# The second gate's matrix product as seven quarter products, with weight sums made by accumulating DMAs

## The chip, the cores and the metric

The kernel runs on one core of a Trainium2 chip. A core has a matrix engine (TensorE, PE in the profile, with its weight loads as PEld), three elementwise engines (VectorE = DVE, ScalarE = ACT, GpSimd = POOL) and a queue engine (SyncE = SP) from which most DMAs are issued. Each engine works off its own queue in order, and engines wait for each other by semaphores. The metric is the device time of one launch in microseconds. Three runs of the kernel before took 667.21, 667.22 and 667.36 us; the median is 667.22 us.

## The reference

A trunk of two layers over 512 tokens of width 1024, in fp32. Layer 0 mixes tokens by neighbourhood attention, layer 1 by latent attention (MLA). Behind each mixer and its output projection stands a gated embedding; a last RMSNorm closes the trunk:

```python
    for i in range(DEPTH):
        xn = rmsnorm(x, norm_g[i])
        y = mixer_na(xn, ...) if i % 2 == 0 else mixer_mla(xn, ...)
        h = x + y
        gate = jax.nn.sigmoid(rmsnorm(h, ple_norm[i]) @ ple_w_gate[i])   # 512x1024 @ 1024x1024
        x = h + gate * (p[i] @ ple_w_proj[i])
    return rmsnorm(x, final_norm)
```

The change is about the product inside the sigmoid, in layer 1.

## The kernel before

**Precision.** An fp32 operand is split into a high part (type fp32r) and the rest, and a product is three matmul passes: high·high, low·high, high·low. A weight piece is 128 rows of 1024 columns (512 KB). `load_w` (line 68) brings it in by three steps: a DMA from SP into `wraw` (L77), a conversion on ScalarE into `whi` (L78), a subtraction on POOL into `wlo` (L79). There are three buffers of each, and during an output projection and the gate behind it a further pool of five pairs of `whi` and `wlo`. Tokens are split on ScalarE (L89) and VectorE (L91), out of PSUM.

**Stages.** In order of time: the first norm and the embeddings `pe = p @ ple_w_proj`, kept in DRAM; layer 0's projections and neighbourhood attention (eight pairs of heads; `project(j+1)` is emitted ahead of `attend(j)`); output projection, first gate, norm; layer 1's compressed projections, MLA heads, output projection; the second gate and the last norm.

**Attention of layer 0.** For a pair of heads, q and k weights are loaded and split, 24 matmuls each, and the PSUM result is copied out by ScalarE (L255, L256 for q) and VectorE (L257, L259). Each head loads a bias table of 192 KB from SP (L317). POOL normalises the softmax rows `ex` (L358), which TensorE then transposes (L369, L371); POOL also does one step of each pair's gating (`u`, L198, and `ol`, L202).

**Output projection** (`out_proj`, line 397): two column halves n, four token tiles t of 128, 24 matmuls of 128x512 each. The result is added to the residual (L409), and `turn_h(t, n)` multiplies it by the gate norm's weights, transposes it on TensorE and splits it into `hnT`; behind a tile's second half, the sum of squares (L110 to L112) gives the row factor `rh`.

**Gate** (`gate_phase`, line 465): for each column half n four weight pieces, and for each of four token tiles 24 matmuls into a PSUM bank: 192 matmuls of 128x512. In layer 1 the last tile's block is cut into two of 256 columns. Behind each block: sigmoid on ScalarE with the row factor as scale (L479), times `pe` (L480), plus the residual (L482) on VectorE, then `done`. In layer 1 `done` gathers the last norm's sum of squares (ScalarE L874 and VectorE L875; for the last 256 columns VectorE L870), multiplies the first half by the norm's weights on POOL (L879), and at a tile's second half takes the power on POOL (L882), scales both halves (VectorE L883, ScalarE L884) and stores (L885, L886).

**PSUM** has eight banks by tag: `mm` 2, `S` 2, `T` 3, `O` 1.

**What sets the order.** The program is emitted in source order; a planner that plays it through with costs of its own then orders each engine's queue, within the dependencies. `issue_after(x)` holds what it wraps behind instruction x in that order.

Of the kernel before, what the change touches and what calls it, by code (L numbers as in the profile page):

```python
# [19 lines left out]
P = 128  # L20
S = 512
# [9 lines left out]
NEARLY = 7  # L31

# [7 lines left out]
class Trunk:  # L40
    def __init__(self, tc, ctx, a, dbg=None):
# [12 lines left out]
        self.small = ec(tc.tile_pool(name="small", bufs=8))  # L54
        self.wx, self.wxn = None, 0
        dram = ec(tc.tile_pool(name="dram", bufs=4, space=bass.MemoryType.DRAM))
        self.spill = [dram.tile([P, D], F32, name=f"spill{t}") for t in range(NT)]
        self.pe = [[dram.tile([P, D], F32, name=f"pe{l}{t}") for t in range(NT)] for l in range(2)]

# [8 lines left out]
    def load_w(self, ap, n, extra=False, parts=1, rest=None, late=None):  # L68
# [4 lines left out]
        hi = pool.tile([P, n if extra else 1024], F32R, name="whi", tag="whi", bufs=self.wxn if extra else 3)  # L73
        lo = pool.tile([P, n if extra else 1024], F32R, name="wlo", tag="wlo", bufs=self.wxn if extra else 3)
# [31 lines left out]
    def inv_rms(self, scratch, src, n):  # L106
# [4 lines left out]
        nc.vector.tensor_scalar(ss, ss, 1.0 / n, EPS, op0=ALU.mult, op1=ALU.add)  # L111
# [3 lines left out]
    def rms(self, dst, src, g, n):  # L115
        rs = self.inv_rms(dst, src, n)
        self.nc.vector.scalar_tensor_tensor(dst, src, rs, g, op0=ALU.mult, op1=ALU.mult)
# [95 lines left out]
    def na_heads(self, pool, xT, zs, oT):  # L213
# [99 lines left out]
    def na_head(self, pool, h, sq, s0, dk, kl, vh):  # L313
# [3 lines left out]
        nc.sync.dma_start(bias, self.a["na_bias"][h])  # L317
# [5 lines left out]
        for half in range(2):  # L323
# [31 lines left out]
            for i in range(2):  # L355
                qt = 2 * half + i
                e = ex[:, ecol(qt)]
                nc.gpsimd.tensor_tensor(out=e, in0=e, in1=rc[:, qt:qt + 1].to_broadcast([P, e.shape[1]]), op=ALU.mult)  # L358
# [126 lines left out]

    def mla_c(self, pool, xT, cT, sets):
# [6 lines left out]
        xh, xl = xT  # L493
        L = lambda s, k, t: s[k // 4][:, k % 4, t * P:(t + 1) * P]
        for part, (w0, wn) in enumerate(((0, 384), (384, 288))):
            ws = [self.load_w(a["mla_c"][part][c], 2 * wn, extra=c == 3) for c in range(4)]
            for t in range(NT):
                ps = self.psum(("mm", "mm", "S", "S", "T", "T", "O", "mm")[part * NT + t])
# [5 lines left out]
        for t in range(NT):  # L504
# [255 lines left out]
    def run(self):  # L760
# [7 lines left out]
        with tc.tile_pool(name="pre", bufs=4, reuse_waits="tile") as pool:  # L768
# [36 lines left out]
            nc.gpsimd.tensor_scalar(ss, ss, 1.0 / D, EPS, op0=ALU.mult, op1=ALU.add)  # L805
            nc.gpsimd.tensor_tensor(out=ss, in0=ss, in1=self.half.to_broadcast([P, NT]), op=ALU.pow)
# [16 lines left out]
        x1T = None  # L823
        for layer in range(2):
            with tc.tile_pool(name=f"out{layer}", bufs=4, reuse_waits="tile") as pool:
                self.wx, self.wxn = pool, 5
# [7 lines left out]
                hnT, rh = {}, {}  # L834

# [15 lines left out]
                if layer == 0:  # L851
                    x1T = ([self.bigtile(f"x1h{g}") for g in range(2)], [self.bigtile(f"x1l{g}") for g in range(2)])

                    def done(t, n, o, w):
                        if n == 0:
                            return
# [143 lines left out]
```

## Time and profile before

| | |
|---|---|
| median of the runs | 667.22 us (667.21 to 667.36) |
| span of the profiled execution | 665.9 us |
| TensorE busy | 657.4 us, 99% |
| ScalarE, POOL, VectorE busy | 407.9, 392.8, 354.8 us |
| moved by DMA | 79.09 MB, mean 119 GB/s |
| second gate, first to last matmul | 614.1 to 658.6 us |

The profile is of one execution. Its span runs from the first to the last recorded work; the device time of a run holds a little more. A busy share says how long an engine had an instruction in work. Matmuls overlap in the engine's pipeline, so a single one has a longer duration than the time by which it advances the queue. In the rows of a timeline the columns are the start, the busy time of the group, the engine, the line, the operation, output and inputs, shapes and the count; a bracket at the end tells the idle time before and what ended it. In a DMA group's row the figures are the count of DMAs, the KB of each and the median microseconds from issue to landing.

### The profile page before, as it was taken

To read this page: it belongs to the slowest core of one execution; us is meant where nothing else is said; L and a number is where in the kernel's file an instruction comes from. 1 tells how busy PE (TensorE), PEld (TensorE's weight loads), DVE (VectorE), ACT (ScalarE), POOL (GpSimd) and SP (SyncE) were. 2 spreads that over 40 slices of the span, in tenths; PEclk is the share of its full clock that TensorE was granted. 3 is DMA by queue.
4 is the path that set the end of the run, shared out by engine and by line. 5 is a ranking of instruction groups with operands and counts; after the bars stand their busy time and mean duration, and the time that the engine had idled before them with its cause. 6 is when DMAs were issued, how large, how long until landed. Compare 5 with 4: busy or idle time off the path is not lost.

```text
span 665.9 us, 9961 instructions
## 1 busy us (share of the span) xinstructions
PE 657.4 (99%) x3467; PEld 560.1 (84%) x3467; DVE 354.8 (53%) x794; ACT 407.9 (61%) x812; POOL 392.8 (59%) x320
## 2 busy tenths in 40 slices
PE   9999999999999999999999999999999999999995
PEld 6888888988988888888899888888888888888885
DVE  6280365736645514544625614888988875145234
ACT  7572586857767742543433635898979887436423
POOL 0395466575575765943044626786959786858410
PEclk9999999999999999999999999999999999999999
DMA  9944223222142236534233335120201223664022
GB/s 327 340 153 136 95 87 94 83 85 99 55 150 76 64 133 262 189 105 138 100 104 110 107 89 168 32 74 24 75 23 64 64 96 111 234 240 159 32 80 95
DMA packets 32386, 79.09 MB, mean 119 GB/s; under 512 B 4177, under 2 KB 8785, under 8 KB 32337
## 3 DMA queue, kind: packets, MB, share of 16 engines
q1 hardware_dynamic: 31904, 77.68, 35.0%
q10 hardware_dynamic: 432, 0.79, 0.3%
q8 instruction: 27, 0.44, 0.3%
q14 instruction: 23, 0.18, 0.1%
HBM read 66.92 MB, written 8.39 MB: 113 GB/s over the span
## 4 chain that ended last, share of the span: by engine, by line
PE 95%; DMA 1%; issue 1%; POOL 1%; DVE 0%; ACT 0%; SPq 0%; POOLq 0%; ACTq 0%
PE ps_mm L102 47%; PE ps_S L102 13%; PE ps_mm L550 6%; PE ps_T L128 6%; PE ps_O L661 4%; PE ps_T L102 3%; PE ps_O L102 3%; PE ps_T L227 2%; PE ps_O L383 2%; PE ps_mm L173 2%; PE ps_T L371 2%; PE ps_S L336 1%; PE ps_S L335 1%; PE ps_O L227 1%; DMA qe<-rl 1%
## 5 line engine op out<-in xcount | busy, mean ns | idle before, releaser
L79 POOL TENSOR_TENSOR wlo<-wraw,whi 128x1024 fp32r<-128x1024 f32 (+5 forms) x106 | 208.2, 1980 | 119.2 <-ACT whi L78 91.2
L78 ACT ACTIVATE whi<-wraw 128x1024 fp32r<-128x1024 f32 (+5 forms) x107 | 92.5, 886 | 86.9 <-PE ps_mm L102 17.8
L646 POOL TENSOR_TENSOR ex<-ex,rc 128x512 f32<-128x512 f32 x64 | 66.2, 1044 | 25.2 <-DVE rc L645 18.1
L102 PE MATMUL ps_mm<-whi,hnT 128*128 128x512 f32 (+1 forms) x272 | 70.2, 378 | 0.0
L102 PEld LDWEIGHTS ps_mm<-whi,hnT 128*128 128x128 f32 x272 | 49.3, 188 | 9.2
L644 ACT ACTIVATE ex<-ps_S,mx 128x512 f32<-128x512 f32 x64 | 44.0, 688 | 11.9 <-DVE mx L642 10.8
L642 DVE TENSOR_REDUCE mx<-ps_S 128x1 f32<-128x512 f32 x64 | 43.7, 683 | 6.9 <-PE ps_S L102 6.2
L91 DVE TENSOR_TENSOR pt_lo<-ps_T,pt_hi 128x512 fp32r<-128x512 f32 x64 | 43.3, 682 | 7.7 <-ACT pt_hi L89 7.3
L358 POOL TENSOR_TENSOR ex<-ex,rc 128x128 f32<-128x128 f32 (+1 forms) x64 | 34.1, 561 | 20.9 <-DVE rc L354 20.9
L102 PE MATMUL ps_mm<-xh,whi 128*128 128x512 f32 x152 | 40.8, 399 | 0.0
L102 PE MATMUL ps_mm<-wlo,hnT 128*128 128x512 f32 (+1 forms) x136 | 40.5, 378 | 0.0
L89 ACT ACTIVATE pt_hi<-ps_T 128x512 fp32r<-128x512 f32 x64 | 37.7, 594 | 4.4 <-PE ps_T L128 4.1
L128 PE MATMUL ps_T<-ident,ex 128*128 128x128 f32 x256 | 38.4, 272 | 0.0
L102 PE MATMUL ps_mm<-xl,whi 128*128 128x512 f32 x152 | 38.2, 390 | 0.0
L102 PE MATMUL ps_mm<-xh,wlo 128*128 128x512 f32 x152 | 38.0, 390 | 0.0
L128 PEld LDWEIGHTS ps_T<-ident,ex 128*128 128x128 f32 x256 | 31.5, 140 | 7.7 <-POOL ex L646 0.4
L102 PEld LDWEIGHTS ps_mm<-xl,whi 128*128 128x128 f32 x152 | 28.4, 188 | 5.8
L102 PEld LDWEIGHTS ps_mm<-xh,wlo 128*128 128x128 f32 x152 | 28.3, 188 | 5.8
L194 DVE TENSOR_TENSOR u<-ps_O,u 64x512 f32<-64x512 f32 x32 | 22.0, 687 | 19.9 <-ACT u L193 19.3
L112 POOL TENSOR_TENSOR rs<-ss,half 128x1 f32<-128x1 f32 x20 | 12.7, 637 | 33.7 <-DVE ss L111 33.6
L480 DVE TENSOR_TENSOR sg<-pe,sg 128x512 f32<-128x512 f32 (+1 forms) x17 | 12.4, 728 | 35.8 <-ACT sg L479 35.8
L352 ACT ACTIVATE ex<-ex,mx 128x128 f32<-128x128 f32 (+1 forms) x64 | 30.3, 474 | 1.9 <-DVE mx L342 1.0
(354 smaller groups left out, 1644.6 us busy)
## 6 DMA issues: line engine op xcount, KB each, us to landing
pe<-pe SPq DMA_DIRECT2D x32, 256.0 KB, 2.8
wraw<-na_qk SPq DMA_DIRECT2D x16, 512.0 KB, 3.3
wraw<-gate SPq DMA_DIRECT2D x16, 512.0 KB, 3.4
wraw<-na_v SPq DMA_DIRECT2D x8, 512.0 KB, 3.3
wraw<-na_o SPq DMA_DIRECT2D x8, 512.0 KB, 3.5
wraw<-mla_z SPq DMA_DIRECT2D x8, 512.0 KB, 3.5
wraw<-mla_o SPq DMA_DIRECT2D x8, 512.0 KB, 3.6
wraw<-na_z SPq DMA_DIRECT2D x6, 512.0 KB, 5.4
```

The lines of the kernel that those rows point to most:

```text
L78: nc.scalar.activation(hi[:, c], raw[:, c], AF.Copy)
L79: f = lambda e, c=c: e.tensor_tensor(out=lo[:, c], in0=raw[:, c], in1=hi[:, c].bitcast(F32), op=ALU.subtract)
L89: self.last_copy = nc.scalar.activation(hi, src, AF.Copy, scale=scale)
L91: nc.vector.tensor_tensor(out=lo, in0=src, in1=hi.bitcast(F32), op=ALU.subtract)
L102: last = self.last_mm = nc.tensor.matmul(out, l, r, start=i == 0, stop=i == n - 1)
L128: self.last_mm = self.nc.tensor.transpose(t[:, i * P:(i + 1) * P], b, self.ident)
L352: self.last_exp = nc.scalar.activation(e, e, AF.Exp, scale=-1.0, bias=mx[:, qt:qt + 1], accum_out=sm[:, qt:qt + 1])
L358: nc.gpsimd.tensor_tensor(out=e, in0=e, in1=rc[:, qt:qt + 1].to_broadcast([P, e.shape[1]]), op=ALU.mult)
L550: self.last_mm = nc.tensor.matmul(PS[key], *terms[i], start=i == 0, stop=i == len(terms) - 1)
L642: nc.vector.reduce_max(mx, sp, axis=AX.X, negate=True)
L644: nc.scalar.activation(ex, sp, AF.Exp, bias=mx, accum_out=sm)
L646: nc.gpsimd.tensor_tensor(out=ex, in0=ex, in1=rc.to_broadcast([P, S]), op=ALU.mult)
```

## The change

With `SEVEN = (1,)` the second gate's product is computed as in Winograd's form of Strassen's method. Tokens (rows, two halves of 256), the inner dimension and the columns are halved; of the eight products of quarters seven remain, of sums of quarters. Numbered 1 to 7 in the code, they run in the order 1, 7, 6, 5, 4, 3, 2. Each is two row halves of 128 with 12 matmuls of 128x512 (inner dimension 512, three passes): 168 in place of 192. For products 1 and 2 the second row half is cut into 256-column pieces.

- **Weight sums.** Products 4 to 7 use sums of weight quarters. Four copies of 1 MB within DRAM (`sums_begin`, SP queue) stand behind a bias load in the first heads of layer 0's attention, and four accumulating DMAs of 1 MB (`sums_add`, issued by POOL, rows of 1 KB) behind normalisations in the next head pairs. The gate then loads 14 pieces of 512 KB (8 before): 14 conversions on ScalarE, 14 subtractions on POOL.
- **Token mixes.** `turn_h` multiplies by a row factor too (`rows`, from tiny operations on POOL and one reciprocal). `keep_half` takes the transposed halves from PSUM: it keeps copies, forms sums and differences of quarters on VectorE, and `operand` splits each of the 14 row halves into high and low part.
- **Partial results.** Products 5 and 3 accumulate in the banks of product 6, and product 2 in those of product 1; ScalarE copies the results of 1 and 6 out in between (`s1`, `s6`), VectorE forms `s17`, and POOL makes two subtractions on `s6`. The blocks behind products 5, 4 and 3 start with one VectorE sum.
- **Order.** The output projection's second half takes the token tiles as 0, 2, 1, 3. The gate's blocks end in another order: tiles 2 and 3 with column half 1, then 0; tiles 0 and 1 with half 1, then 0, so that `done` now takes the halves in the order in which they come. The extra pool holds five pairs under one tag.

```diff
+    def sums_begin(self, layer):
+        q = lambda n, c: self.a["gate"][layer, n, c:c + 2].rearrange("c p n -> (c p) n")
+        w = self.quarter[layer] = {1: q(0, 0), 2: q(0, 2), 3: q(1, 2), "f": q(1, 0)}
+        for p, src in ((7, "f"), (5, 1), (6, 1), (4, 2)):
+            nc.sync.dma_start(t[p], w[src])
+    def sums_add(self, layer, step):
+        for p, src in {0: ((7, q[3]), (5, q["f"])), 1: ((6, t[7]),), 2: ((4, t[6]),)}[step]:
+            self.nc.gpsimd.dma_start(t[p], src, accum_op=ALU.add, max_dma_last_dim=1024)
...
             attend(j)
+            for l in SEVEN:
+                if j == 0:
+                    with self.tc.issue_after(self.last_bias.ins):
+                        self.sums_begin(l)
+                elif j < 4:
+                    with self.tc.issue_after(self.last_norm.ins):
+                        self.sums_add(l, j - 1)
...
+    def operand(self, p, i, x, lo=None):
+        nc.scalar.activation(t[:, i, :], x, AF.Copy)
+        (lo or nc.vector).tensor_tensor(out=t[:, 2 + i, :], in0=x, in1=t[:, i, :].bitcast(F32), op=ALU.subtract)
...
+    def keep_half(self, t, n, ps):
+        i = t % 2
+        ac, c = self.F[:, i, :], self.F[:, 2 + i, :]
+        if t < 2:
+            self.operand(1 + n, i, ps)
+            nc.scalar.activation(self.B[i] if n else ac, ps, AF.Copy)
+        elif n == 0:
+            nc.scalar.activation(c, ps, AF.Copy)
+            nc.vector.tensor_tensor(out=ac, in0=ac, in1=ps, op=ALU.subtract)
+            self.operand(7, i, ac)
+        else:
+            nc.vector.tensor_tensor(out=ac, in0=ac, in1=ps, op=ALU.add)
+            nc.vector.tensor_tensor(out=c, in0=c, in1=ps, op=ALU.subtract)
+            nc.scalar.activation(self.Dd[i], ps, AF.Copy)
+    def mixed(self, p):
+        for i in range(2):
+            if p == 3:
+                self.nc.vector.tensor_tensor(out=self.B[i], in0=self.B[i], in1=self.F[:, i, :], op=ALU.subtract)
+            self.operand(p, i, {6: self.F[:, i, :], 5: self.F[:, 2 + i, :], 3: self.B[i], 4: self.Dd[i]}[p])
...
+    def gate_seven(self, pool, layer, rh, res, after):
+        order = (1, 7, 6, 5, 4, 3, 2)
+        for p in order[:3]:
+            prep(p)
+        self.mixed(6)
+        for k, p in enumerate(order):
+            if k + 3 < len(order):
+                prep(order[k + 3])
+            if 0 < k < 4:
+                self.mixed(order[k + 2])
+            for i in range(2):
+                cuts = parts if layer == 1 and i == 1 and p < 3 else whole
...
+                    m = [(x[:, 2 * s + i, k * P:(k + 1) * P], W[p][k // 2][r][:, k % 2 * S + o:k % 2 * S + o + wd])
+                         for c in range(2) for s, r in ((0, 0), (1, 0), (0, 1)) for k in (2 * c, 2 * c + 1)]
+                    for j, (l, r) in enumerate(m):
+                        nc.tensor.matmul(ps[:, :wd], l, r, start=j == 0 and p in (1, 7, 6, 4),
+                                         stop=j == 11 and p not in (1, 6, 5), skip_group_check=True)
+                    if p == 1:
+                        nc.scalar.activation(s1[i][:, o:o + wd], ps[:, :wd], AF.Copy)
+                    elif p == 2:
+                        finish(i, 0, pool.tile([P, S], F32, name="g", tag="hg", bufs=3)[:, :wd], ps[:, :wd], o, wd)
+                    elif p == 7:
+                        nc.vector.tensor_tensor(out=s17[i], in0=ps, in1=s1[i], op=ALU.add)
+                    elif p == 6:
+                        nc.scalar.activation(s6[i], ps, AF.Copy)
+                    elif p == 5:
+                        quarter(2 + i, 1, ps, s17[i], ALU.subtract)
+                        nc.gpsimd.tensor_tensor(out=s6[i], in0=s17[i], in1=s6[i], op=ALU.subtract)
+                    elif p == 4:
+                        quarter(2 + i, 0, ps, s6[i], ALU.add)
+                    else:
+                        quarter(i, 1, ps, s1[i], ALU.subtract)
...
-            for t in range(NT):
-                ps = self.psum(("mm", "mm", "S", "S", "T", "O", "mm", "mm")[n * NT + t])
+            for u, t in enumerate((0, 2, 1, 3) if n and self.wxn > 5 else range(NT)):
+                ps = self.psum(("mm", "mm", "S", "S", "T", "O", "mm", "mm")[n * NT + u])
```

More of the change, by code (lines that the diff above doesn't have):

```diff
@@ L31 @@
 NEARLY = 7
+SEVEN = (1,)
 def win(t, r0, r1, off, dims):
@@ L54, in __init__ @@
         self.small = ec(tc.tile_pool(name="small", bufs=8))
+        self.rows = [[self.const.tile([P, NT], F32, name=f"row{n}{l}") for n in "abcd"] for l in range(2)]
         self.wx, self.wxn = None, 0
@@ L58, in __init__ @@
         self.pe = [[dram.tile([P, D], F32, name=f"pe{l}{t}") for t in range(NT)] for l in range(2)]
+        self.quarter = {}
+        self.sums = [{p: dram.tile([2 * P, D], F32, name=f"sum{l}{p}") for p in (4, 5, 6, 7)} for l in range(2)]
     def bigtile(self, name):
@@ L503, in mla_c @@
         slab_l = pool.tile([P, S], F32R, name="slab_l", tag="slab", bufs=2)
-        for t in range(NT):
+        for t in toks:
             c = cs[t]
@@ L851, in run @@
                 if layer == 0:
-                    x1T = ([self.bigtile(f"x1h{g}") for g in range(2)], [self.bigtile(f"x1l{g}") for g in range(2)])
                     def done(t, n, o, w):
-                        if n == 0:
+                        if t not in seen:
+                            seen.add(t)
                             return
```

159 lines of the change are left out of this document (129 added, 30 removed).

## The prediction

> **What bounds the kernel now.** I read the page first (span, busy shares, chain), then the chain in order of time for the end, then a window over the second gate.
>
> ```profile
> span 665.9 us, 9961 instructions
> PE 657.4 (99%) x3467; PEld 560.1 (84%) x3467; DVE 354.8 (53%) x794; ACT 407.9 (61%) x812; POOL 392.8 (59%) x320
> PE 95%; DMA 1%; issue 1%; POOL 1%; DVE 0%; ACT 0%; SPq 0%; POOLq 0%; ACTq 0%
> ```
>
> TensorE is busy 99% of the span and is 95% of the chain; the other engines stand near 55%. So what counts is matmul time, and any hole that new work tears into it.
>
> ```profile
> 621.06 31.78 PE ps_mm L102 x140
> 655.10 0.73 ACT sq L874 x2
> 656.70 3.88 issue
> 661.19 0.75 DVE r L883
> ```
> ```profile
> core 0: us, PE busy (x) PEld busy (x) DVE busy (x) ACT busy (x) POOL busy (x), PEclk, DMA share, GB/s
> 5.00:15.00 10.00, 9.70 (x42) 7.66 (x42) 9.80 (x16) 9.07 (x16) 0.00 (x0) 1.00 1.04 377
> 52.00:66.00 14.00, 14.00 (x64) 11.58 (x63) 0.00 (x0) 3.46 (x4) 7.57 (x4) 1.00 0.40 135
> 614.11:658.60 44.49, 44.46 (x221) 37.64 (x219) 16.58 (x32) 16.92 (x32) 13.66 (x11) 1.00 0.19 66
> ```
>
> The chain's long row gives 31.78/140 = 0.227 us for one matmul of 128x512 in the second gate. The last window is that gate up to its last matmul: TensorE 44.46 of 44.49 us, granted clock 1.00, VectorE, ScalarE and POOL busy 17, 17 and 14 us. The end is a chain from the last matmul (658.6) to 665.9, 7.3 us. The profiled run spans 665.9, and the median of the runs is 667.2, so I add 1.3 us to a span.
>
> **The change part by part.**
>
> *Matmuls.* Eight tokens-by-half blocks of 24 become seven products of two row halves with 12 each: 192 → 168. The blocks cut into 256 columns make up one whole block's length before (24 pairs) and the same after (two blocks of 12 pairs), so they cancel. 24 × 0.227 = **−5.45 us**, all of it on the path.
>
> *End.* The rows after the last matmuls:
>
> ```profile
> 655.10 0.63 ACT L874 ACTIVATE sq<-r 128x512 f32<-128x512 f32 x1 [1.54 <-DVE r L482]
> 655.63 0.19 ACT L874 ACTIVATION_READ_ACCUMULATOR sq<-r 128x1 f32 x1
> 656.73 0.73 ACT L884 ACTIVATE r<-r,rs 128x512 f32<-128x512 f32 x1 [0.52 <-POOL rs L882]
> 656.73 0.75 DVE L883 SCALAR_TENSOR_TENSOR r<-r,rs,gn 128x512 f32<-128x512 f32 x1
> 658.61 0.47 ACT L479 ACTIVATE sg<-ps_mm,rs 128x256 f32<-128x256 f32 x1 [0.19 <-PE ps_mm L102]
> ```
>
> The last block's own steps (L479 onward) are unchanged. Before it, the neighbour token's block ended 24 matmuls (5.4 us) earlier, now 12 (2.7 us), so its square (0.63 + 0.19) can sit in ScalarE's queue ahead of the last sigmoid. I take that one square, **+0.8 us**. Bounds: 0 if it is through in time, 2.3 if the neighbour's scaling (0.73, 0.75) stands there as well.
>
> *The four 1 MB copies in DRAM.* They are issued on SP in the first layer's attention, behind the second head's bias and so ahead of weights: three before the k weights of head pair 0, one before the q weights of pair 1.
>
> ```profile
> 46.13 0.33 SPq L77 DMA_DIRECT2D wraw<-na_qk  x1
> 46.68 1.28 SPq L317 DMA_DIRECT2D bias<-na_bias  x3
> wraw<-na_qk SPq DMA_DIRECT2D x16, 512.0 KB, 3.3
> spill<-r SPq DMA_DIRECT2D x4, 512.0 KB, 2.7
> qo<-rl SPq DMA_DIRECT2D x8, 64.0 KB, 2.0
> 64.64 1.06 ACT L78 ACTIVATE whi<-wraw 128x1024 fp32r<-128x1024 f32 x1 [4.38 <-PE ps_O L227]
> 71.84 0.59 ACT L255 ACTIVATE sa<-ps_mm 64x512 fp32r<-64x512 f32 x1 [0.43 <-PE ps_mm L102]
> 73.79 0.69 DVE L259 SCALAR_TENSOR_TENSOR sb<-ps_mm,sb 64x512 fp32r<-64x512 f32 x1
> 77.08 1.98 PE L102 MATMUL ps_mm<-xh,whi 128*128 128x512 f32 x8
> ```
>
> 448 KB more take 1.3 us more: 345 GB/s, and 1.8 us fixed. Call a copy c. If one queue is served in order, pair 1's q weights land at 47.5 (after two of the bias issues) + 1.1 (two bias tables, 0.56 each) + 4c + 1.5 (k weights) + 0.56 (third table) + 1.5 + 1.8 = 54.0 + 4c. Their conversion ran at 64.64 and may slip about 3.0 us: behind it on ScalarE stand 0.43 us of idle time and the steps that empty a PSUM bank, done at 74.48, wanted at 77.08. So the deadline is 67.7, met up to c = 3.4. No copy within DRAM is in the trace. Lower end c = 3.0 (1 MB at 345 GB/s; 377 in the first window when all engines are full): nothing late. Upper end 6.1 (reading and writing in turn): 78.4, 10.7 us of idle TensorE. [...] In all, the loss is 4(c − 3.4).
>
> [...]
>
> *The four accumulating DMAs* are issued by POOL: two behind the pair of ex rows that ends at 117.48, one at 128.4, one at 156.9. POOL's queue stands still while it writes their 1024 rows each.
>
> ```profile
> 116.29 1.19 POOL L358 TENSOR_TENSOR ex<-ex,rc 128x256 f32<-128x256 f32 x2
> 118.37 2.40 POOL L79 TENSOR_TENSOR wlo<-wraw,whi 128x1024 fp32r<-128x1024 f32 x1 [0.89 <-ACT ph L89]
> 122.37 0.97 POOL L358 TENSOR_TENSOR ex<-ex,rc 128x128 f32<-128x128 f32 x2 [1.60 <-DVE rc L354]
> 124.79 0.27 PE L369 MATMUL ps_T<-ident,ex 128*128 128x128 f32 x1
> 130.62 1.29 POOL L198 TENSOR_TENSOR u<-u,z 128x512 f32<-128x512 f32 x1 [2.21 <-DVE u L194]
> 132.87 1.30 POOL L202 TENSOR_TENSOR ol<-u,oh 128x512 fp32r<-128x512 f32 x1 [0.96 <-ACT oh L201]
> 160.08 1.01 POOL L358 TENSOR_TENSOR ex<-ex,rc 128x128 f32<-128x128 f32 x2 [0.80 <-DVE rc L354]
> 164.40 0.27 PE L369 MATMUL ps_T<-ident,ex 128*128 128x128 f32 x1
> ```
>
> Behind the pair stand wlo, then the ex that TensorE transposes at 124.79; its slack is 0.89 + 1.60 + 1.45 = 3.9 us. Behind the third stand u and ol (2.21 + 0.96 = 3.2 us); behind the fourth the ex that ends at 161.09 and is transposed at 164.40 (0.80 + 3.3 = 4.1 us). An SP issue of 128 rows takes 0.33 us; with the same for any DMA the pair is 0.7, with one such step for each 128 rows 2.6 each and 5.2 for the pair, 1.3 us too long. I take 0 with 1.3 kept; a gain is excluded, as this is work added. Their transfers run on a queue of their own, and weight conversions there wait for TensorE's buffers, not for loads:
>
> ```profile
> L78 ACT ACTIVATE whi<-wraw 128x1024 fp32r<-128x1024 f32 (+5 forms) x107 | 92.5, 886 | 86.9 <-PE ps_mm L102 17.8
> ```
>
> *Weights and mixes in the gate.* Fourteen weight pieces for eight, and more operand work.
>
> ```profile
> 593.73 11.85 POOL L79 TENSOR_TENSOR wlo<-wraw,whi 128x1024 fp32r<-128x1024 f32 x5 [1.60 <-ACT whi L78]
> 618.61 2.39 POOL L79 TENSOR_TENSOR wlo<-wraw,whi 128x1024 fp32r<-128x1024 f32 x1
> 624.12 1.29 POOL L879 TENSOR_TENSOR r<-r,gn 128x512 f32<-128x512 f32 x1 [3.12 <-ACT sq L874]
> 639.63 1.28 POOL L879 TENSOR_TENSOR r<-r,gn 128x512 f32<-128x512 f32 x1 [4.16 <-ACT sq L874]
> L91 DVE TENSOR_TENSOR hnT<-ps_T,hnT 128x512 fp32r<-128x512 f32 x4 | 2.7, 688 | 2.9 <-ACT hnT L89 2.9
> L89 ACT ACTIVATE hnT<-ps_T 128x512 fp32r<-128x512 f32 x4 | 2.3, 587 | 0.0
> ```
>
> POOL: 6 × 2.39 + 2 subtractions × 1.28 = 17 us more. VectorE: 22 more half-tile steps (6 low parts, 8 mixes, 8 sums behind products) × 0.69 = 15 us. ScalarE: 19 copies (14 of token operands, 5 of products) × 0.59, and 6 more weight pieces × 1.06 = 18 us. On top of 14, 17 and 17 us that makes 31, 32 and 35 in about 39 us of matmuls, and part runs ahead during the output projection. POOL is the tightest: before, eight pieces were through at 621.0. Six more end no sooner than 621.0 + 14.3 + 2.6 + 4 × 1.28 = 643.0; the last product starts at 614.1 + 6 × 5.45 = 646.8. The third product's operands, the first that need mixes after the last transposes, have two products (10.9 us) for about four VectorE and three ScalarE steps (4.5 us). I take 0; bounds 0 and, if POOL stayed 4 us idle more than I count, some 3 us.
>
> **Sum.** −5.45 + 0.8 + 1.1 + 0 + 0 = −3.55: span 662.35, time **663.7 us**.
>
> **The rivals.**
>
> *A, the other side: the copies are slow.* The deadline of pair 1's q weights decides: the loss 4(c − 3.4) eats the 4.65 us left above c = 4.6. At the upper end, 6.1, it is 10.7: 673.3 us. For it: nothing shows both sides of a copy overlapping. Against: loads of whole tiles and the spill to DRAM are both under 3.5 us for 512 KB. Chance 0.20, more than half of it close to the point of decision. [...]
>
> *B, POOL writes descriptors slowly.* With G for each DMA the stalls are 2G − 3.9, G − 3.2 and G − 4.1, together 4G − 11.2; beside the copies' 1.1 the gain is gone from G = 3.7. At G = 5, 8.8 us: 672.5. Nothing speaks for it but that no such DMA is in the trace; against it the 0.33 us row. Chance 0.08.
>
> *C, the gate starves.* The change does not do what it says: the 24 matmuls leave, but the products wait for POOL's pieces. If none ran ahead, 14 × 2.39 + 2.6 + 5.1 = 41.2 us against 38.1 of matmuls, +3.1: 666.8. Against: POOL's rows at 593.73. Chance 0.10.
>
> **How the numbers follow.** The forecast's case holds 0.62, its own range 661.8 (no tail, copies hidden) to 666.0 (tail 2.3, copies at c = 3.9). Measured runs differ by 0.02%; 0.2% (1.3 us) is about what can be told from no change. Faster: 0.62 and a little of C, 0.64. Same: parts of A and C, 0.11. Slower: the rest of A and B, 0.25. The range 661.5 to 669.0 takes in C and A up to c = 5.0, and leaves out A's far end and B's, about 0.16.
>
> **What would show it.** Gate: 168 whole matmuls' worth, TensorE without holes. Tail: 8.1 us after the last matmul. Copies: their landing, and TensorE idle between 77 and 90 us (pair 1) if c is over 3.4. POOL: length of its DMA issues, transposes late after 118, 129 and 160 us. I am wrong if the 5.45 us is there in the gate and lost in the first 170 us.

## The result, and the profile after

| | before | changed |
|---|---|---|
| median of the runs | 667.22 us (667.21 to 667.36) | 670.1 us (669.8 to 670.96) |
| ratio to before | | 1.0045 [1.0031, 1.0059] |
| span of the profiled execution | 665.9 us | 668.0 us |
| second gate, first to last matmul | 614.1 to 658.6 us | 613.6 to 653.6 us |
| from the last matmul to the end | 7.3 us | 14.4 us |

The change makes the kernel slower by 0.45%; 663.7 us was predicted. The gate's last matmul ends 5.0 us earlier, and the kernel ends 2.1 us later: what follows the last matmul has grown by 7.1 us. The profiled execution of the changed kernel took 669.8 us, 1.8 us more than its span; it is the shortest of four, whose spans run from 668.0 to 669.2 us. The medians lie 2.9 us apart, these two spans 2.1.

The page of the changed kernel, its busy shares, and windows over the gate and its end:

```profile
PE 652.5 (98%) x3443; PEld 555.5 (83%) x3443; DVE 383.1 (57%) x817; ACT 422.3 (63%) x837; POOL 421.4 (63%) x340
PE 91%; DVE 2%; POOL 2%; issue 2%; DMA 1%; ACT 1%; POOLq 0%; DVEq 0%
```
```profile
614.00:630.00 16.00, 15.90 (x84) 13.29 (x83) 15.90 (x17) 11.39 (x21) 13.38 (x6) 1.00 0.50 171
630.00:640.00 10.00, 10.00 (x46) 8.28 (x45) 3.04 (x5) 6.57 (x9) 8.57 (x5) 1.00 0.24 86
640.00:650.00 10.00, 9.88 (x44) 7.87 (x43) 9.02 (x11) 4.27 (x9) 5.37 (x4) 1.00 0.19 65
650.00:656.00 6.00, 3.61 (x28) 3.29 (x26) 5.77 (x12) 4.89 (x11) 2.92 (x4) 1.00 0.42 147
656.00:662.00 6.00, 0.00 (x0) 0.00 (x0) 5.96 (x13) 3.16 (x9) 3.74 (x3) 0.55 0.26 96
```

The columns of the windows are those of the prediction's: TensorE, weight load, VectorE, ScalarE, POOL. TensorE is busy 35.78 of the 36 us from 614 to 650 at a granted clock of 1.00, so it isn't starved. VectorE (third figure) is busy only 3.04 of the 10 us between 630 and 640, and then almost without a gap to 662, when TensorE has long ended. On the chain TensorE fell from 95% to 91%; VectorE rose from 0 to 2% and POOL from 1 to 2%.

VectorE's groups from 589 us to the end, shapes kept apart, show why its row is so long:

```profile
L539 DVE TENSOR_TENSOR X<-mix,X 128x512 fp32r<-128x512 f32 x6 | 9.1, 1523 | 2.0 <-ACT X L538 2.0
L599 DVE TENSOR_TENSOR r<-r,g 128x512 f32<-128x512 f32 x7 | 8.2, 1177 | 0.0
L1016 DVE SCALAR_TENSOR_TENSOR hg<-r,rowb,gp 128x512 f32<-128x512 f32 x5 | 5.7, 1152 | 2.2 <-PE ps_T L139 2.2
L604 DVE TENSOR_TENSOR g<-ps_S,s 128x512 f32<-128x512 f32 x4 | 2.7, 681 | 4.6 <-PE ps_S L634 4.6
L560 DVE TENSOR_TENSOR mix<-mix,ps_T 128x512 f32<-128x512 f32 x2 | 1.4, 680 | 2.1 <-PE ps_T L139 2.1
```

All are steps over one 128x512 tile. Those with an operand from PSUM (`ps_S`, `ps_T`) take 0.68 us; the three groups whose two large operands lie in SBUF take 1.15 to 1.5 us on the average. From 640 on six of them are long, and each of the six meets a POOL step. VectorE's rows first, then POOL's:

```profile
640.75 1.02 DVE L597 TENSOR_TENSOR g<-pe,g 128x512 f32<-128x512 f32 x1 [3.08 <-ACT g L594]
641.81 2.77 DVE L599 TENSOR_TENSOR r<-r,g 128x512 f32<-128x512 f32 x1
646.03 1.22 DVE L597 TENSOR_TENSOR g<-pe,g 128x512 f32<-128x512 f32 x1 [0.19 <-ACT g L594]
650.85 1.12 DVE L599 TENSOR_TENSOR r<-r,g 128x512 f32<-128x512 f32 x1
656.38 1.63 DVE L599 TENSOR_TENSOR r<-r,g 128x512 f32<-128x512 f32 x1
659.54 1.42 DVE L599 TENSOR_TENSOR r<-r,g 128x256 f32<-128x256 f32 x1
```
```profile
639.94 1.28 POOL L650 TENSOR_TENSOR s<-s,s 128x512 f32<-128x512 f32 x1
641.18 2.85 POOL L590 TENSOR_TENSOR wlo<-wraw,whi 128x1024 fp32r<-128x1024 f32 x1
645.41 1.29 POOL L1064 TENSOR_TENSOR r<-r,gn 128x512 f32<-128x512 f32 x1 [1.38 <-ACT sq L1060]
649.95 1.47 POOL L1064 TENSOR_TENSOR r<-r,gn 128x512 f32<-128x512 f32 x1 [3.25 <-ACT sq L1060]
655.98 1.49 POOL L1064 TENSOR_TENSOR r<-r,gn 128x512 f32<-128x512 f32 x1 [2.32 <-ACT sq L1060]
658.91 1.77 POOL L1064 TENSOR_TENSOR r<-r,gn 128x512 f32<-128x512 f32 x1 [1.44 <-ACT sq L1060]
```

Each of the six steps from 640.75 to 659.54 begins while POOL has one in work, and ends 0.3 to 0.6 us behind POOL's end. Against 0.68 us (0.41 for the 256-column one) they cost 0.34 + 2.09 + 0.54 + 0.44 + 0.95 + 1.01 = 5.4 us, on an engine that has hardly any idle time left. That is one part of the 7.1 us. The other is that VectorE starts late:

```profile
636.99 0.69 DVE L604 TENSOR_TENSOR g<-ps_S,s 128x512 f32<-128x512 f32 x1 [4.64 <-PE ps_S L634]
```
```profile
637.62 1.06 ACT L589 ACTIVATE whi<-wraw 128x1024 fp32r<-128x1024 f32 x1 [3.40 <-POOL s L650]
638.70 1.28 ACT L594 ACT_TABLE_LOAD   x1
640.00 0.72 ACT L594 ACTIVATE g<-g,rs 128x512 f32<-128x512 f32 x1
```

The first sum behind a product starts at 636.99, after 4.64 us of waiting for TensorE: the planner put half of product 4 ahead of product 5. Then the first sigmoid stands behind the last weight conversion and a table load until 640.00. By then 13.6 us of matmuls are left, and all eight blocks of outputs are still to be multiplied and added.

### The profile page after: what moved, and what is told of

Its sections match the earlier page's. It is cut to its first block, busy times and chain, and to the rows that moved or that the text cites. A ratio compares the mean times of both kernels' runs of the same rounds, so it can differ in the third digit from the quotient of the medians.

```text
span 668.0 us, 10021 instructions
## 1 busy us (share of the span) xinstructions
PE 652.5 (98%) x3443; PEld 555.5 (83%) x3443; DVE 383.1 (57%) x817; ACT 422.3 (63%) x837; POOL 421.4 (63%) x340
## 4 chain that ended last, share of the span: by engine, by line
PE 91%; DVE 2%; POOL 2%; issue 2%; DMA 1%; ACT 1%; POOLq 0%; DVEq 0%
PE ps_mm L107 42%; PE ps_S L107 13%; PE ps_mm L721 6%; PE ps_T L139 6%; PE ps_O L832 4%; PE ps_T L107 3%; PE ps_O L107 3%; PE ps_T L238 2%; PE ps_O L402 2%; PE ps_mm L184 2%; PE ps_T L390 2%; PE ps_S L354 1%; PE ps_S L353 1%; DVE r L599 1%; PE ps_O L238 1%
## 5 line engine op out<-in xcount | busy, mean ns | idle before, releaser
L84 POOL TENSOR_TENSOR wwlo<-wraw,wwhi 128x1024 fp32r<-128x1024 f32 (+5 forms) x93 | 178.6, 1934 | 106.3 <-ACT wwhi L83 91.4
L83 ACT ACTIVATE wwhi<-wraw 128x1024 fp32r<-128x1024 f32 (+5 forms) x94 | 79.1, 863 | 74.4 <-PE ps_mm L107 18.3
L107 PE MATMUL ps_mm<-xh,wwhi 128*128 128x512 f32 x152 | 40.9, 399 | 0.0
L590 POOL TENSOR_TENSOR wlo<-wraw,whi 128x1024 fp32r<-128x1024 f32 x14 | 36.4, 2619 | 3.2 <-ACT whi L589 3.2
L107 PE MATMUL ps_mm<-xl,wwhi 128*128 128x512 f32 x152 | 38.3, 391 | 0.0
L107 PE MATMUL ps_mm<-xh,wwlo 128*128 128x512 f32 x152 | 38.0, 390 | 0.0
L107 PE MATMUL ps_mm<-wwhi,hnT 128*128 128x512 f32 x128 | 35.0, 392 | 0.0
L107 PEld LDWEIGHTS ps_mm<-xl,wwhi 128*128 128x128 f32 x152 | 28.4, 188 | 5.9
L370 ACT ACTIVATE ex<-ex,mx 128x128 f32<-128x128 f32 (+1 forms) x64 | 30.2, 474 | 1.8 <-DVE mx L360 0.8
L107 PE MATMUL ps_S<-ke,qe 96*128 96x512 f32 x96 | 28.9, 407 | 0.0
L107 PE MATMUL ps_S<-ko,qo 128*128 128x512 f32 x96 | 28.9, 409 | 0.0
```

Of the source, the lines that this page charges most:

```text
L83: nc.scalar.activation(hi[:, c], raw[:, c], AF.Copy)
L84: f = lambda e, c=c: e.tensor_tensor(out=lo[:, c], in0=raw[:, c], in1=hi[:, c].bitcast(F32), op=ALU.subtract)
L107: last = self.last_mm = nc.tensor.matmul(out, l, r, start=i == 0, stop=i == n - 1)
L590: nc.gpsimd.tensor_tensor(out=lo, in0=raw, in1=hi.bitcast(F32), op=ALU.subtract)
```

## The experiments

Two theories stood at first. **P**: VectorE and POOL hold each other up when both read SBUF, and that stretches the end. **Q**: VectorE's steps are long for a reason of their own (their tiles, their waits). The expectations also name **N**: the number of blocks that are left for the last 17 us. Out of it came **O**: the order of the products, which starts the blocks late.

### The two engines alone

A kernel of its own with nothing but rows of steps on VectorE and POOL over tiles in SBUF and PSUM, of which this is the core; it computes nothing of the reference.

```python
section(2, 12, 6, dss, gtt)   # VectorE: two SBUF operands; POOL: 128x1024 subtraction
section(3, 24, 7, dps, gtt)   # VectorE: one operand in PSUM; the same POOL row
section(5, 24, 7, dss, gset)  # POOL only writes
section(6, 24, 24, dss, lambda o, f: gtt(o, f, 256))
```

> A kernel of its own that computes nothing of the reference: VectorE and POOL run additions and subtractions on fixed tiles, in sections. Theory P (VectorE and POOL exclude each other while a VectorE instruction reads two SBUF tiles and a POOL instruction reads SBUF): VectorE 128x512 from two SBUF tiles takes 0.69 us alone and about 2.4 us beside POOL's 128x1024 subtraction, 1.3 beside POOL's 128x512, about 0.7 to 0.8 beside POOL's 128x256; with one operand in PSUM 0.69 throughout; beside a POOL memset 0.69. Rival Q (the rows of the changed kernel are long for another reason, such as a wait for data that the record counts as busy): 0.69 in all sections.

Its timeline, with rows of VectorE and then of POOL:

```profile
10.25 16.09 DVE L38 TENSOR_TENSOR d<-x,x 128x512 f32<-128x512 f32 x7
26.97 3.59 DVE L41 TENSOR_TENSOR d<-pt,x 128x512 f32<-128x512 f32 x5
38.60 0.68 DVE L38 TENSOR_TENSOR d<-x,x 128x512 f32<-128x512 f32 x1
```
```profile
11.42 13.65 POOL L47 TENSOR_TENSOR p<-x,x 128x1024 f32<-128x1024 f32 x5
27.76 9.60 POOL L47 TENSOR_TENSOR p<-x,x 128x1024 f32<-128x1024 f32 x4
```

Beside POOL's subtraction a step of VectorE with two SBUF operands takes 16.09 / 7 = 2.30 us on the average, alone 0.68. The average takes in the first step, beside a shorter POOL step, and the last, which begins behind POOL's row; the five between them take 2.71 us each. One of the five, and the POOL step beside it:

```profile
16.91 2.67 POOL L47 TENSOR_TENSOR p<-x,x 128x1024 f32<-128x1024 f32 x1
17.41 2.71 DVE L38 TENSOR_TENSOR d<-x,x 128x512 f32<-128x512 f32 x1
```

VectorE's step ends 0.54 us behind POOL's, as in the changed kernel. With one operand in PSUM a VectorE step takes 0.69 us beside the same row, and POOL 2.40 us (9.60 / 4, whether or not VectorE is at work) instead of 2.73 (13.65 / 5). So the two take turns by whole instructions in these rows, and P holds; Q, which gave 0.69 in every section, falls. Beside POOL's steps of 512 and of 256 columns VectorE took 1.63 and 1.1 us, more than the 1.3 and the 0.7 to 0.8 expected.

### The copies and the accumulating DMAs alone

The kernel before, with `sums_begin` and `sums_add` and their calls added; their sums are not used.

```diff
+            for l in SEVEN:
+                if j == 0:
+                    with self.tc.issue_after(self.last_bias.ins):
+                        self.sums_begin(l)
+                elif j < 4:
+                    with self.tc.issue_after(self.last_norm.ins):
+                        self.sums_add(l, j - 1)
```

> The kernel before with the four copies and the four accumulating DMAs added at the places of the change, and their sums not used. Theory H (hidden): span 665.9 us, first gate and second gate as before. Theory K (the DMAs cost a part of the 2.9 us): TensorE idle near 77 us or near 118 to 160 us. The changed kernel's runs are 1.8 to 2.1 us longer than their spans and those of before 1.3; if the DMAs issued by POOL are the reason, this kernel takes 667.7 us with a span of 665.9, and if not, 667.2.

Measured: 667.64 us against 667.66, ratio 1.0001 [0.9992, 1.001], span 665.9. All eight DMAs cost nothing that can be told. The 7 us are not theirs. The kernel before had a median span of 665.9 us beside it, so it too took 1.8 us more than its span here: the DMAs issued by POOL are not the reason for such a difference, and the 1.3 us that the prediction added is no constant.

### POOL's subtractions left out, or cut

First the 14 low parts are left out, and the matmuls read the high part in their place:

```diff
-                nc.gpsimd.tensor_tensor(out=lo, in0=raw, in1=hi.bitcast(F32), op=ALU.subtract)
-                W[p].append((hi, lo))
+                W[p].append((hi, hi))
```

> The changed kernel without POOL's 14 subtractions for low parts of the gate's weights; the matmuls read the high part in their place (a wrong product, as many matmuls). Theory P (POOL's long instructions hold up VectorE's): VectorE's steps between two SBUF tiles in the gate fall from 1.2 to 1.7 us to 0.69, the end after the last matmul from 14.5 to 8 to 9 us: 664 us. Theory N (not the neighbour but the number: seven of eight blocks end in the gate's last 17 us, with 20 us of VectorE work at 0.69): the end stays at 11 us or more: 667 us or more. Both: between.

Then they stay, each cut into four of 256 columns, so that a VectorE step has a shorter POOL step beside it:

```diff
-                nc.gpsimd.tensor_tensor(out=lo, in0=raw, in1=hi.bitcast(F32), op=ALU.subtract)
+                for s in [slice(i * 256, (i + 1) * 256) for i in range(4)]:
+                    nc.gpsimd.tensor_tensor(out=lo[:, s], in0=raw[:, s], in1=hi[:, s].bitcast(F32), op=ALU.subtract)
```

> The changed kernel with each of POOL's 14 subtractions in the gate cut into four of 256 columns, the result unchanged. Theory P: a VectorE step waits for at most one short POOL instruction, some 0.7 us in place of 2.4; about half of the gap to the kernel without them comes back, 666 to 668 us. Theory N: no change, 670 us, or slower by POOL's fixed cost for each of 42 more instructions.

Left out: 667.96 us, ratio 1.0005 [0.9996, 1.0015], span 666.5, the end 12.7 us. That is 1.7 us of the 7.1 us: P alone had expected 664 us and an end of 8 to 9 us, N 667 us or more and an end of 11 us or more, as measured. VectorE's first sum still starts at 638.24, and POOL's `r` times `gn` still meets VectorE's steps: two sums with the residual (L598) take 2.38 us from 646.89 on, beside a POOL step from 647.26 to 648.72.

Cut: 676.03 us, ratio 1.0131 [1.0114, 1.0148], worse, and outside what either theory gave (666 to 668, or 670 us). Rows of the timeline, of VectorE, POOL and TensorE, and then a window behind them:

```profile
643.43 4.86 DVE L598 TENSOR_TENSOR g<-pe,g 128x512 f32<-128x512 f32 x1 [6.59 <-ACT g L595]
642.18 5.56 POOL L591 TENSOR_TENSOR wlo<-wraw,whi 128x256 fp32r<-128x256 f32 x8
649.67 2.08 PE L635 MATMUL ps_S<-whi,X 128*128 128x512 f32 x4 [4.95 <-DVE g L605]
```
```profile
650.00:656.00 6.00, 6.00 (x15) 4.65 (x15) 5.61 (x10) 2.99 (x7) 2.58 (x2) 0.51 0.32 106
```

A single VectorE step stood 4.86 us, from the second of POOL's eight short steps to the end of the eighth: VectorE didn't get in between them here, though it did in the kernel of the two engines alone (1.1 us a step). What decides that is open. TensorE then waited 4.95 us for a PSUM bank, and afterwards ran at a granted clock of 0.51 for 6 us, with 15 matmuls in that window.

### One cause at a time, with POOL at work

Three single edits of the changed kernel, and all three together. The blocks behind products 4, 3 and 2 keep their values in the PSUM bank of their product, so that VectorE reads one operand from PSUM:

```diff
-            x = pool.tile([P, S], F32, name="g", tag="hg", bufs=3)
+            x = pool.tile([P, S], F32, name="g", tag="hg", bufs=3) if keep else ps
...
-                        finish(i, 0, pool.tile([P, S], F32, name="g", tag="hg", bufs=3)[:, :wd], ps[:, :wd], o, wd)
+                        finish(i, 0, ps[:, :wd], ps[:, :wd], o, wd)
```

> The changed kernel with the blocks behind products 4, 3 and 2 kept in their PSUM banks: the sum, the sigmoid and the product with pe are written over the bank, so that none of these VectorE steps reads two SBUF tiles (product 5's two blocks stay as they are). Theory P: the product and residual rows of these blocks go from 0.8 to 1.2 us to 0.69, some 4 us off VectorE's row of work at the end, ratio to before about 0.999. Theory N (VectorE's number of steps and their late start): under 1 us, ratio 1.003 to 1.0045.

The products are held in their order 1, 7, 6, 5, 4, 3, 2:

```diff
+                        with self.tc.issue_after(prev) if prev is not None and j == 0 else nullcontext():
+                            mm = nc.tensor.matmul(ps[:, :wd], l, r, start=j == 0 and p in (1, 7, 6, 4),
...
+                    prev = mm.ins
```

> The changed kernel with TensorE's products held in the order 1, 7, 6, 5, 4, 3, 2 (in the changed kernel the planner put half of product 4 ahead of product 5, and began 6 ahead of 7). Theory N: product 5's first block ends near 633 us in place of 636.8, VectorE's last row of work starts up to 4 us earlier and ends as much earlier: ratio 0.999 to 1.001. Theory P: no change, 1.0045, or worse if the mixes of product 5 come too late. Theory W (the first sigmoid waits in ScalarE's queue behind the last weight conversion, whose load waits for POOL): the first sum is earlier and the first sigmoid is not, still near 640 us: 1.003 to 1.0045.

The table of the sigmoid is loaded early, by a tiny sigmoid behind the first copy of product 1:

```diff
+                        if i == 0:
+                            with self.tc.issue_after(cp.ins):
+                                nc.scalar.activation(self.small.tile([P, 1], F32, name="dm", tag="dm", bufs=1), self.half, AF.Sigmoid)
```

> The changed kernel with one sigmoid of 128x1 right behind the copy of product 1's first half, so that the table load of 1.28 us falls there and not ahead of the first block's sigmoid. If VectorE's wait for that sigmoid (3.08 us in the changed kernel) passes on to the end, 1.2 us less: ratio 1.0025. If not, 1.0045.

And the three edits together:

> The three edits together: blocks in PSUM, the order held, the table loaded early; result unchanged. If the causes add, 3 to 4 us + 0 to 4 + 1.2 of the 7.2 us that the end is longer than before come back: ratio 0.993 to 0.997. If all of them shorten the same wait, as one of them alone.

| | median, us (before beside it) | ratio | span, us | last matmul ends | end, us |
|---|---|---|---|---|---|
| blocks in PSUM | 669.11 (667.89) | 1.0019 [1.0009, 1.0028] | 666.8 | 653.7 | 13.1 |
| order held | 673.53 (667.89) | 1.0079 [1.0062, 1.0096] | 672.5 | 661.2 | 11.3 |
| table early | 674.31 (667.89) | 1.0098 [1.0083, 1.0113] | 672.5 | 658.2 | 14.3 |
| all three | 671.33 (667.89) | 1.0051 [1.0036, 1.0066] | 669.7 | 658.0 | 11.7 |

Only the first helps, by less than the 4 us that P gave: its end is 13.1 us. With the order held the end does become shorter, 11.3 us in place of 14.4, but the last matmul comes 7.6 us later: product 5 comes earlier than its operands, which VectorE forms beside POOL. A row of VectorE, the row of TensorE that waits for it, and a window:

```profile
634.50 2.25 DVE L539 TENSOR_TENSOR X<-mix,X 128x512 fp32r<-128x512 f32 x1
634.04 1.22 PE L636 MATMUL ps_S<-whi,X 128*128 128x512 f32 x2 [3.50 <-DVE X L539]
```
```profile
630.00:640.00 10.00, 6.50 (x17) 4.78 (x16) 10.00 (x8) 4.59 (x6) 9.30 (x5) 0.66 0.35 107
```

VectorE is busy all 10 us and TensorE waits 3.50 us for it, again followed by a lower clock: 0.66 over the window, and 0.43 us for a matmul from 634.04 to 640.01, where it took 0.23 before the wait. The planner's own order had covered this lateness. With the early table, the load stands at 631.50 ahead of two weight conversions in ScalarE's queue, and the first sigmoid starts at 644.03, later than without. Its gate also began 3 us later, at 616.56, and so did that of the three edits together; TensorE's rows are a little slower there from about 270 us on: 1700 matmuls between 280 and 606 us, where the other kernels with the copies had 1706 to 1709. What causes that drift is open, and these two runs are no clean test of the table.

### The order and the PSUM blocks, with POOL's subtractions left out

The low parts are left out as above and the order is held; then the blocks are kept in PSUM too.

> The kernel without POOL's subtractions for low parts in the gate (the matmuls read the high part instead, a wrong product), and with the products held in the order 1, 7, 6, 5, 4, 3, 2. With POOL at work that order was slower than the changed kernel, since VectorE's steps for product 5 waited for POOL. Theory N: without POOL the order pays, product 5's first block ends near 634 us, VectorE's last row of work starts 4 us earlier, the end 3 to 4 us: ratio 0.996 against 1.0005 without the order. Theory P alone: no difference from the kernel without the low parts, 1.0005.

> The same with the blocks behind products 4, 3 and 2 kept in PSUM, which takes the last meetings of VectorE and POOL away (POOL's multiplications by the norm's weights): 1 to 2 us less than the kernel with the order alone, ratio 0.993 to 0.995, which is the 5.45 us of matmuls less 1 to 2 us of a longer end. If the row of VectorE's steps (20 us) still ends last, over 0.997.

Measured 666.95 us, ratio 0.9989 [0.998, 0.9999], and 663.52 us, 0.9937 [0.9923, 0.9952]; the ends are 11.5 and 8.6 us, the first sum with the order held at 634.25. The first lies between what N and P gave, the second where it was expected. With POOL's long steps gone the held order helps by some 1 us (the intervals of the two ratios just touch), where it harmed before, and with PSUM blocks as well 5.8 of the 7.1 us are back. So the 7.1 us are for the most part POOL and VectorE holding each other up, together with blocks that start late; with POOL's long steps at work, the held order, alone or with the others, did not bring the gain.

### A kernel that computes everything

The low parts of the first six weight pieces stay on POOL, those of the other eight are formed by VectorE; order held, blocks in PSUM. In the second kernel POOL also takes the residual sums of tiles 2 and 3.

```diff
-                nc.gpsimd.tensor_tensor(out=lo, in0=raw, in1=hi.bitcast(F32), op=ALU.subtract)
+                (nc.gpsimd if pieces <= 6 else nc.vector).tensor_tensor(out=lo, in0=raw, in1=hi.bitcast(F32), op=ALU.subtract)
```

> A version with the right result: POOL makes the low parts of the first six weight pieces, VectorE of the other eight (1.22 us each, as in the kernel of its own), products in order, blocks in PSUM. If VectorE and POOL may not work at the same time on SBUF, the faster one alone does it sooner: VectorE has 8 x 1.22 = 9.8 us more to do and loses 10 to 12 us of waits. Ratio 0.995 to 0.999. If VectorE's row of work only gets longer: above 1.003.

> The version before with the residual sums of tiles 2 and 3 (four steps of 128x512) on POOL. VectorE's row at the end is 2.8 us shorter; POOL's steps are 1.28 each and meet few VectorE steps with two SBUF tiles. If the row ends last: 1 to 3 us faster than the version before. If POOL's steps then wait for each other or hold up VectorE: the same or slower.

Measured: 663.74 us, ratio 0.9941 [0.9924, 0.9959], and 663.48 us, 0.9936 [0.9921, 0.9951]. Both are faster than before and after, by a little more than the 0.995 to 0.999 expected of the first; between them there is no difference. Groups of the first of them, VectorE and then POOL:

```profile
L590 DVE TENSOR_TENSOR wlo<-wraw,whi 128x1024 fp32r<-128x1024 f32 x8 | 10.5, 1328 | 1.6 <-PE ps_T L139 1.6
L599 DVE TENSOR_TENSOR r<-r,ps_T 128x512 f32<-128x512 f32 x2 | 1.4, 678 | 0.0
```
```profile
L590 POOL TENSOR_TENSOR wlo<-wraw,whi 128x1024 fp32r<-128x1024 f32 x6 | 15.2, 2556 | 0.0
L653 POOL TENSOR_TENSOR s<-s,s 128x512 f32<-128x512 f32 x2 | 6.2, 3113 | 8.1 <-ACT s L650 8.1
```

VectorE takes over 10.5 us of work and still ends earlier: a low part costs it 1.33 us, POOL 2.56. The first sum starts at 633.52, and 7.9 us follow the last matmul (652.7 to 660.6). POOL is now the one that is held: its two subtractions on `s6`, 1.29 us each in the changed kernel, take 3.11 on the average. With 1.29 for the second, the first took 4.93, by an estimate from the 6.2 us of both, beside a row of five VectorE steps with two SBUF operands (628.05 to 632.74).

### What each edit gives, with the whole computation

Three more runs on one chip: the low parts moved alone; with PSUM blocks, the order not held; and the changed kernel again.

> The changed kernel with one edit: the low parts of weight pieces 7 to 14 of the gate are subtracted on VectorE instead of POOL; order of the matmuls and the sums' tiles stay. Theory P (VectorE and POOL hold each other up where both read SBUF, and that is what stretches the end): with the longest POOL steps gone from the last 25 us, VectorE's steps with two SBUF operands fall from 1.2 to 1.7 us towards 0.7 to 0.9 us, and this one edit takes a good part of the 7.1 us: end about 10.5 us, ratio to the kernel before 0.996 to 0.999. Theory O (the late first sum, set by the order that the planner gives to the products, is the larger part): first sum still near 637, end 12 to 13 us as where the low parts were left out, ratio 1.000 to 1.003.

> The last kernel and one more edit: the blocks behind the products keep their sigmoid's output in the PSUM bank of their product, so that VectorE's steps read one operand from PSUM; the matmuls' order is not held. Theory P: the remaining meetings with POOL (its r times gn) go as well: VectorE's steps 0.68 to 0.75 us, end about 8.5 to 9.5 us, ratio 0.994 to 0.996, the same as with the order held (0.994). Theory O: without the held order VectorE starts late and is busy without a gap to the end: end 10.5 to 12 us, ratio 0.997 to 1.000.

> The changed kernel beside the two others on one chip. Both theories: 1.003 to 1.006 of the kernel before, end near 14 us.

| | median, us (before: 667.71) | ratio | first sum | end, us |
|---|---|---|---|---|
| changed kernel again | 670.57 | 1.0048 [1.0036, 1.0061] | 637.52 | 14.4 |
| low parts moved | 668.6 | 1.0014 [1.0005, 1.0023] | 640.84 | 13.3 |
| and blocks in PSUM | 665.33 | 0.9967 [0.9956, 0.9979] | 636.71 | 10.1 |
| and order held (above, another chip, before: 667.79) | 663.74 | 0.9941 [0.9924, 0.9959] | 633.52 | 7.9 |

With the low parts moved alone, VectorE's and POOL's groups and two of VectorE's rows:

```profile
L599 DVE TENSOR_TENSOR r<-r,g 128x512 f32<-128x512 f32 x7 | 5.8, 838 | 0.0
L1064 POOL TENSOR_TENSOR r<-r,gn 128x512 f32<-128x512 f32 x4 | 6.1, 1517 | 14.2 <-ACT sq L1060 14.2
```
```profile
633.81 5.68 DVE L590 TENSOR_TENSOR wlo<-wraw,whi 128x1024 fp32r<-128x1024 f32 x3
640.84 0.69 DVE L604 TENSOR_TENSOR g<-ps_S,s 128x512 f32<-128x512 f32 x1 [1.35 <-PE ps_S L634]
```

The sums with the residual (L599) fell from 1.18 to 0.84 us, as P expects; what is left of the waiting comes from POOL's `r` times `gn`, which is itself at 1.52 us, as in the changed kernel (1.29 to 1.77), where it took 1.28 before the change. Yet the end is 13.3 us, a little over the 12 to 13 of O: VectorE now begins its first sum 3.3 us later than in the changed kernel beside it. It forms three low parts first, then waits 1.35 us for TensorE. The PSUM blocks take 3.2 us more off the end; the second kernel's ratio, 0.9967, lies between what P (0.994 to 0.996) and O (0.997 to 1.000) gave, its end of 10.1 us too. Holding the order then takes another 2.2 us. So order is a part of its own, but it paid only where POOL's long steps were gone from VectorE's side. The three shares, 1.1, 3.2 and 2.2 us, are each from one profiled execution; in the medians the same steps give 2.0, 3.3 and 1.7 us, and the intervals of the last two ratios just overlap. They hold for this sequence of the edits; in another they are others (PSUM blocks first: 1.3 us).

## Why the prediction was wrong

**Matmuls, −5.45: right within 1 us.** The gate takes 40.0 us from first to last matmul instead of 44.5, and begins 0.5 us earlier: the last matmul ends at 653.6 instead of 658.6, −5.0 us. TensorE idles in the gate for about 0.2 us.

**End, +0.8 with bounds 0 and 2.3: this step failed; it measured +7.1.** It looked at the last two blocks and at ScalarE alone: one square or one scaling more in front of the last sigmoid. What ends the kernel now is VectorE's queue. The step took for granted that the blocks before the last are done in time, as they were before, where one block ended every 5.45 us. In the new order all eight begin at 636.99 or later, in the last 16.6 us of the gate, and the chain behind each (sum, sigmoid, product, residual) is long. And where the prediction priced VectorE's steps, among the weights and mixes, it took 0.69 us for each, from a row with an operand in PSUM, though most of the steps at the end have two operands in SBUF, and six of them met a step of POOL. That the two together are what was missing is shown by the runs above: with the order held, the blocks in PSUM and POOL's long steps gone from the last weight pieces, the end is 8.6 us where the low parts are left out and 7.9 us where VectorE forms them, against 7.3 before.

The row that would have told it was in the trace of before. There, early in the first layer, a row of VectorE's steps with two SBUF operands runs beside POOL's own; VectorE's row and then POOL's:

```profile
39.39 7.26 DVE L817 TENSOR_TENSOR xl<-xT,xh 128x512 fp32r<-128x512 f32 x4
38.58 4.72 POOL L817 TENSOR_TENSOR xl<-xT,xh 128x512 fp32r<-128x512 f32 x3
```

7.26 / 4 = 1.8 us a step, where the prediction used 0.69.

**Weights and mixes, 0 with bounds 0 and 3: right for TensorE, wrong as a sum.** The prediction had POOL 31, VectorE 32 and ScalarE 35 us busy in 39, and called POOL the tightest. From 614 to 656 the windows give POOL 30.2, VectorE 33.7 and ScalarE 27.1. No product waited for its pieces, so rival C did not occur. But the sums of busy time were used to say only that TensorE is fed; that VectorE's part lay at the far end of the stretch, 14.8 us of it between 640 and 656 and 6.0 more from 656 to 662, when TensorE has ended, was not asked.

**Copies, +1.1, a c of about 3.7 by 4(c − 3.4): the path was right, the term was mis-sized.** No run shows this c or the 1.1 us that rest on it: the copies took 2.8 to 2.9 us, and the changed kernel's profiled run lost 0. What a copy takes can be read from the landings. The second and the third copy of the changed kernel were issued at 49.64 and 50.26 us; from issue to landing they took:

```profile
sum<-gate SPq DMA_DIRECT2D x1, 8.2
sum<-gate SPq DMA_DIRECT2D x1, 10.4
```

In full, the first three landed at 54.87, 57.80 and 60.66 us, the k weights at 62.39, the fourth copy at 65.16 and the q weights of pair 1 at 67.64. So c is 2.8 to 2.9 us, below the lower end of 3.0 at which the prediction had nothing late. Its 54.0 was too small in turn: 67.64 less four copies is 56.2, as the first copy was issued at 48.49 instead of 47.5 and the rest of the row took longer too. The two errors nearly cancel: 54.0 + 4c would ask for c = 3.4, and that the sum comes out near the measured time is luck. The q conversion of pair 1, row of the changed kernel, then the same row and TensorE's from the kernel with the low parts moved, whose first copy was issued at 49.40 and whose c is 2.8 to 2.9 us as well:

```profile
67.74 1.06 ACT L83 ACTIVATE wwhi<-wraw 128x1024 fp32r<-128x1024 f32 x1 [4.19 <-DMA wraw<-na_qk]
```
```profile
69.77 1.06 ACT L83 ACTIVATE wwhi<-wraw 128x1024 fp32r<-128x1024 f32 x1 [4.14 <-DMA wraw<-na_qk]
78.54 2.08 PE L107 MATMUL ps_mm<-xh,wwhi 128*128 128x512 f32 x8 [1.67 <-DVE sb L270]
```

Over the 15 profiled kernels with the copies the conversion started between 67.30 and 69.77; up to 68.34 TensorE idled 0.07 us at most there, and at 69.21, 69.37 and 69.77 it idled 0.87, 0.90 and 1.67 us, in the place foreseen. So the deadline is a good half microsecond later than the predicted 67.7, and the loss was 0 in the profiled run of the changed kernel. Each copy moved its 1 MB in 2.8 to 2.9 us, some 370 GB/s. Rival A did not occur.

**Accumulating DMAs, 0 with bounds 0 and 1.3: right.** POOL's rows in the changed kernel:

```profile
117.33 2.86 POOL L527 DMA_DIRECT2D sum<-gate  x2
128.83 1.30 POOL L527 DMA_DIRECT2D sum<-sum  x1 [0.47 <-DMA sum<-gate]
```

G is 1.3 to 1.4 us, between the 0.33 and 2.6 taken as ends, and far from the 3.7 of rival B. The run with the copies and these DMAs alone agrees.

None of the three rivals happened. The slower side was reached by a mechanism that was not among them: the gate's elementwise work is hidden behind TensorE as long as TensorE runs, and its rest stands behind the last matmul. The sign of being wrong that the prediction named, a gain in the gate that is lost in the first 170 us, was not the one that came: the gain was there in the gate and was lost behind it.

## What to carry to other kernels

When matmuls are taken away, ask of every other engine not only whether its busy time fits beside the rest, but when its last piece of work can start and how much of it is left then; that is what stands behind the last matmul. Price a VectorE step by where its operands lie and by what POOL does meanwhile (0.68 us alone, 2.71 here with two SBUF operands beside POOL's subtraction). Keep one operand in PSUM (0.69 beside that subtraction), or give the work to the faster engine (a low part took VectorE 1.33 us, POOL 2.56), before cutting POOL's work into smaller steps, which took this kernel from 1.0045 to 1.0131 of the time before. An order that a planner chose may cover a late operand: holding another one by hand took the ratio from 1.0045 to 1.0079 here, and from 1.0005 to 0.9989 once POOL's subtractions were left out.

## What the runs showed of the hardware

- In the kernel of the two engines alone, VectorE steps with two SBUF operands and POOL's subtraction took turns by whole instructions: 0.68 us became 2.71 (2.30 on the average of the row), and POOL's own step went from 2.40 to 2.73. With one operand in PSUM neither was slowed (0.69, 2.40). Beside six POOL steps that only write, twelve VectorE steps took 8.71 us, 0.73 each, in a row that begins beside a POOL step that reads.
- POOL was held too: by the estimate above a 1.29 us step took 4.93 us beside a row of five VectorE steps with two SBUF operands.
- A copy of 1 MB within DRAM, issued by SP in a row with others, took 2.8 to 2.9 us of that queue; an accumulating DMA of 1 MB in rows of 1 KB took 1.3 to 1.4 us of POOL's queue.
- Shorter POOL steps were no remedy here. In the kernel with two engines alone VectorE took 1.1 us beside 128x256 steps, but in the gate it stood 4.86 us through six of them and the rest of one more.
- Two pauses of TensorE were followed by slow matmuls. After 4.95 us without work TensorE ran at a granted clock of 0.51 for 6 us. For 6 us after 3.50 us without work a matmul took 0.43 us instead of 0.23, and the window with that wait showed 0.66. The pauses of 0.87 to 1.67 us near 78 us left the clock at 1.00.
